# Output projection of a hybrid decoder layer as seven block products instead of eight, with weight sums made by adding transfers

## The chip, the cores and the metric

The kernel runs on one core of a Trainium2 chip. TensorE (PE in the profile) multiplies, VectorE (DVE), ScalarE (ACT) and GpSimd (POOL) work on vectors, SyncE (SP) issues transfers. The metric is the device time of one execution in microseconds (us), lower is better. POOL can issue transfers too, and those may add to what lies at their destination.

## The reference

One layer with 512 tokens of width 1024, float32. What matters here is the end of the mixer and the start of the MLP:

```python
merged = jax.nn.sigmoid(gate_attn) * attn + jax.nn.sigmoid(gate_conv) * conv
x = x + merged @ w_out[l]

hmid = jnp.square(jax.nn.relu(rms_norm(x, norm_mlp_g[l]) @ w_ff1[l]))
x = x + hmid @ w_ff2[l]
```

`attn` is a projection by `w_attn_o`, `conv` one by `w_conv_out`; `merged` is 512 x 1024, `w_out` 1024 x 1024, `w_ff1` 1024 x 4096 and `w_ff2` 4096 x 1024.

## The kernel before

Every float32 product is done in three passes of a rounded format (fp32r): a matrix is split in a high half (ACT copies it with rounding) and a low half (the difference, a subtraction on DVE or POOL), and high x high, high x low and low x high are summed in PSUM. A weight chunk thus needs one ACT and one DVE or POOL instruction of 128 x 1024 for each 512 KB that a transfer brings.

The order of the work is written out by hand. `at(pos, fn, ...)` files a step under a position; all steps are sorted by it and issued in that order, and each engine runs its own part of them as an in-order queue. One unit of position is six matmuls of 512 columns. `WO` is where the projection by `w_attn_o` starts, `WC` that by `w_conv_out`, `W0` the output projection by `w_out`, `M0` the MLP.

- **Merge** (`wc_evac`, L629 to L634). For each 128 of the 1024 features, DVE multiplies and adds in PSUM (L630, L631), ACT rounds half of it to the high half `mT["h"]` (L632), DVE makes the low half (L633).
- **Output projection** (L1006 to L1077). It is plain: first the left 512 output columns for all four token tiles at once (`wout_first`), then the right ones tile by tile (`wout_second`), 96 matmuls each. The weights come in four chunks in the ring of the buffer tag `raw`; the low halves are made by POOL for the first two pieces and by DVE afterwards (L465).
- **Residual and norm.** `residual` adds the projection to `x1` on DVE, `residual_square` sums the squares on ACT, `x2_norm` (L1039) makes the root of the mean and the normed tile `u` on DVE, with short instructions of one column in between (L1041, L150, L127 to L130) and one long one (L1045). `x2_trans` transposes `u` on PE, `x2_keep` copies it to `cx`, the MLP's operand. The tiles `x1` are loaded at `WO + 3` (L993).
- **MLP** (L1089 to L1341). Eight phases, `w_ff1` and `w_ff2` in turn for a quarter of the hidden width. Each phase is a 1024 x 1024 product in 2 x 2 blocks of 512, in Winograd's form with seven products instead of eight. `piece_hi` and `piece_lo` (L1134 to L1139) split the weight blocks on ACT and DVE, `products` (L1152) issues the matmuls, `op_sum`, `op_hi` and `op_lo` make the sums and halves of the other operand, `row_add` (L1171) adds a product to `x1`. Weight sums are made by DVE (`block_sum`, L1130) or by transfers that add (`fetch_add`, L1116, issued by POOL). Phase 0 starts with products 1 and 2, which need token tiles 0 and 1 only, then product 7, which needs all four.

Four weight blocks are held (`raw` in `tl`) and four pieces (`ph`, `pl`); piece `n` goes to place `n % 4`, so its high half waits until TensorE has finished with piece `n - 4`.

Of the kernel before, what the change touches and what calls it, by code (L numbers as in the profile page):

```python
# [53 lines left out]
def tile_hybrid_block(  # L54
# [220 lines left out]
    kw = [gpool.tile([P, KD, 256], F32R, name=f"kw{i}", tag="gate", bufs=2) for i in range(2)]  # L275
# [188 lines left out]
    def split_lo(u):  # L464
        eng = ve if u in wout_uses[2:] else ge  # L465
        eng.tensor_tensor(out=pieces[u][1], in0=piece_of(u), in1=pieces[u][0].bitcast(F32), op=ALU.subtract)
# [147 lines left out]
    for name, c0, tag, res in (("ta", GLU_END, "gate", ta), ("tc", GA_END, "kT", tcv)):  # L614
        at(b + 3.9, gate_tiles, name, tag, res)
# [7 lines left out]
    aTh, mT = {}, {}  # L623
    M_SHAPE = [P, 2, S]
# [4 lines left out]
    def wc_evac(ps, m):  # L629
        ve.scalar_tensor_tensor(out=ps, in0=tcv[m], scalar=1.0, in1=ps, op0=ALU.add, op1=ALU.mult)  # L630
        ve.tensor_tensor(out=ps, in0=ta[m], in1=ps, op=ALU.add)  # L631
        se.activation(mT["h"][:, m, :], ps, AF.Copy, scale=0.5)  # L632
        ve.scalar_tensor_tensor(out=mT["l"][:, m, :], in0=ps, scalar=0.5, in1=mT["h"][:, m, :].bitcast(F32),  # L633
                                op0=ALU.mult, op1=ALU.subtract)  # L634
# [320 lines left out]
    def merge_tiles():  # L955
        for n in "hl":
            mT[n] = keep.tile([P, KD, S], F32R, name=f"mT{n}", tag="act", bufs=2)

    at(WC, merge_tiles)


    W0 = WC + 4 * KD
    M0 = W0 + 32
    tl = {}

    def open_tail():
# [4 lines left out]
        tl["raw"] = [pool.tile([P, 4, S], F32, name=f"block{i}") for i in range(2)]  # L971
        for n in "hl":
            tl["p" + n] = [pool.tile([P, 2, S], F32R, name=f"piece{n}")]
        tl["u2"] = pool.tile([P, 2, D], F32, name="u2", tag="aOh")
# [6 lines left out]
        for n in "hl":  # L981
            tl["wout" + n] = pool.tile([P, KD, S], F32R, name=f"wout1{n}", tag="xS" + n)
# [7 lines left out]
    def load_x1():  # L990
        for t in range(NT):
            x1_t = keep.tile([P, D], F32, name=f"x1_{t}", tag="at", bufs=4)
            nc.sync.dma_start(x1_t, x[t * P:(t + 1) * P, :])  # L993
            x1.append(x1_t)

    at(WO + 3, load_x1)
# [9 lines left out]
    def wout_mm(acc, k, t, wh, wl):  # L1006
        cols = slice(t * P, (t + 1) * P)
        mm_M(acc, mT["h"][:, k, cols], mT["l"][:, k, cols], wh, wl, k == 0, k == KD - 1)

    def wout_first(u, i, j):  # L1010
        if i + j == 0:
            tl["acc"] = [bank(f"ps_wo0_{t}") for t in range(NT)]
        wh, wl = pieces[u]
        for t in range(NT):
            wout_mm(tl["acc"][t], 2 * i + j, t, wh[:, j, :], wl[:, j, :])

    def wout_second(t, i):
        if i == 0:
            tl["acc", t] = bank(f"ps_wo1_{t}")
        for k in (2 * i, 2 * i + 1):  # L1020
            wout_mm(tl["acc", t], k, t, tl["wouth"][:, k, :], tl["woutl"][:, k, :])

    def wout_hi(m):
        se.copy(tl["wouth"][:, 2 * m:2 * m + 2, :], raws[wout_late[m // 2]][:, 2 * (m % 2):2 * (m % 2) + 2, :])

    def wout_lo(m):
        ks = slice(2 * m, 2 * m + 2)
        ve.tensor_tensor(out=tl["woutl"][:, ks, :], in0=raws[wout_late[m // 2]][:, 2 * (m % 2):2 * (m % 2) + 2, :],
                         in1=tl["wouth"][:, ks, :].bitcast(F32), op=ALU.subtract)

    def residual(t, half, acc):
        cols = slice(half * S, half * S + S)
        ve.tensor_tensor(out=x1[t][:, cols], in0=x1[t][:, cols], in1=acc, op=ALU.add)

# [4 lines left out]
    def x2_norm(t):  # L1039
# [3 lines left out]
        rs = rsqrt_root(root[t], mean_eps(ss, D, 1, f"m{t}"), 1, f"m{t}")  # L1043
# [393 lines left out]
```

## Time and profile before

| | us |
|---|---|
| median of 3 runs | 768.29 |
| the runs | 766.93, 768.29, 1067.66 |
| span of the profiled execution | 766.8 |
| output projection starts | 401.49 |
| MLP's phase 0 starts | 448.44 |
| MLP's phase 2 starts | 528.87 |
| merge's eight instructions each, ACT L632 and DVE L633 | 0.60 and 0.69 |

The profiled execution's span is 0.1 us below the lowest run and 1.5 below the median; the third run was disturbed. Starts are counted from the span's start. In the profile's rows a name like `ps_x<-xSh,pieceh` says what an instruction writes and reads, with buffer numbers left out; L1163 is the line of the matmuls of a `w_ff1` phase, L1168 that of a `w_ff2` phase.

### The profile page before, as it was taken

The page shows a single profiled execution, that of the slowest core. Times are in us where ns is not written, and L with a number is a line of the kernel's source. Part 1 is how long each engine was busy: PE and PEld are TensorE (multiplying, and loading weights), DVE is VectorE, ACT ScalarE, POOL GpSimd, SP SyncE. Part 2 cuts the span into 40 slices and gives each one's busy share as a digit, 9 for nine tenths or more (in the row PEclk, how much of TensorE's full clock was granted, in tenths as well). Part 3 has the DMA queues.
Part 4 walks back from the last instruction along what each step waited for, and adds up shares of the span by engine and source line. Part 5 has one row for each costly group of instructions (what it writes and reads, how often), then busy time and mean ns, then how long its engine had stood idle before and what let it go on. Part 6 is the DMA issues. An engine that isn't in the chain of part 4 may idle for free.

```text
span 766.8 us, 11628 instructions
## 1 busy us (share of the span) xinstructions
PE 758.6 (99%) x4468; PEld 667.5 (87%) x4468; DVE 604.4 (79%) x926; ACT 439.8 (57%) x697; POOL 275.8 (36%) x215
## 2 busy tenths in 40 slices
PE   9999999999999999999999999999999999999997
PEld 8989989898888888888888899979998899889986
DVE  5467978898878888888436678899779977998696
ACT  7445457667566656348325367754675467536761
POOL 1454978958675475524440002210121011101110
PEclk9999999999999999999999999999999999999999
DMA  7441051313223113533228207983588359844772
GB/s 260 157 146 56 1 165 31 108 56 120 73 78 117 56 57 109 168 108 101 104 70 302 82 29 140 218 204 98 150 208 193 110 135 218 179 129 119 166 157 109
DMA packets 65870, 97.48 MB, mean 127 GB/s; under 512 B 3524, under 2 KB 36340, under 8 KB 65814
## 3 DMA queue, kind: packets, MB, share of 16 engines
q1 hardware_dynamic: 56566, 78.91, 30.9%
q0 software_dynamic: 9248, 17.83, 13.7%
q8 instruction: 35, 0.57, 0.3%
q14 instruction: 21, 0.17, 0.1%
HBM read 94.60 MB, written 2.12 MB: 126 GB/s over the span
## 4 chain that ended last, share of the span: by engine, by line
PE 85%; DVE 5%; ACT 3%; DMA 3%; POOL 2%; issue 2%; POOLq 0%; ACTq 0%; DVEq 0%
PE ps_x L1163 10%; PE ps_z L1168 8%; PE ps_y L1163 5%; PE ps_y L1168 4%; PE ps_x L1168 3%; PE ps_z L1163 2%; DMA block<-in_w_ff_dram 2%; PE ps_ta L498 2%; PE ps_ta L500 2%; PE ps_wo L198 2%; PE ps_wo L199 2%; PE ps_wo L197 2%; PE ps_ta L499 2%; PE ps_wc L500 2%; PE ps_wc L499 2%; PE ps_wc L498 2%
## 5 line engine op out<-in xcount | busy, mean ns | idle before, releaser
L1138 DVE TENSOR_TENSOR piecel<-block,pieceh 128x1024 fp32r<-128x1024 f32 x112 | 136.2, 1223 | 33.5 <-ACT pieceh L1135 33.4
L1135 ACT CAST pieceh<-block 128x1024 fp32r<-128x1024 f32 x112 | 116.0, 1050 | 71.4 <-DVE block L1132 21.4
L1118 POOL DMA_DIRECT2D block<-in_w_ff_dram x34 | 41.3, 1249 | 296.9 <-DVE piecel L1138 173.1
L800 DVE SCALAR_TENSOR_TENSOR cv<-h,wcol,cv 128x512 f32<-128x512 f32 x208 | 147.7, 748 | 0.5
L1163 PE MATMUL ps_x<-xSh,pieceh 128*128 128x256 f32 x192 | 54.1, 282 | 0.4 <-ACT c L1182 0.4
L1163 PE MATMUL ps_x<-xSl,pieceh 128*128 128x256 f32 x192 | 53.9, 281 | 0.0
L1163 PE MATMUL ps_x<-xSh,piecel 128*128 128x256 f32 x192 | 53.9, 281 | 0.0
L709 ACT ACTIVATE s<-s,negm 128x257 f32<-128x257 f32 (+1 forms) x64 | 30.4, 480 | 16.5 <-DVE negm L701 16.5
L1168 PE MATMUL ps_z<-piecel,aSh 128*128 128x512 f32 x96 | 37.8, 394 | 0.9 <-DVE piecel L1138 0.8
L733 DVE TENSOR_TENSOR pTl<-ptp,pTh 128x512 fp32r<-128x512 f32 x28 | 19.4, 691 | 23.0 <-ACT pTh L729 23.0
L1168 PE MATMUL ps_z<-pieceh,aSh 128*128 128x512 f32 x96 | 37.5, 390 | 0.0
L1168 PE MATMUL ps_z<-pieceh,aSl 128*128 128x512 f32 x96 | 37.4, 390 | 0.0
L1132 DVE TENSOR_TENSOR block<-block,block 128x1024 f32<-128x1024 f32 x30 | 36.6, 1224 | 0.8 <-DMA block<-in_w_ff_dram 0.4
L1163 PEld LDWEIGHTS ps_x<-xSh,piecel 128*128 128x128 f32 x192 | 36.8, 192 | 0.0
L197 PE MATMUL ps_q<-wh_q,uTh 128*128 128x256 f32 x128 | 36.6, 286 | 0.0
L1163 PEld LDWEIGHTS ps_x<-xSh,pieceh 128*128 128x128 f32 x192 | 36.0, 188 | 0.6 <-ACT c L1182 0.6
L199 PE MATMUL ps_q<-wh_q,uTl 128*128 128x256 f32 x128 | 36.2, 283 | 0.0
L198 PE MATMUL ps_q<-wl_q,uTh 128*128 128x256 f32 x128 | 36.2, 283 | 0.0
L1163 PEld LDWEIGHTS ps_x<-xSl,pieceh 128*128 128x128 f32 x192 | 36.1, 188 | 0.0
L792 POOL TENSOR_TENSOR side<-side,tap 128x512 f32<-128x512 f32 x24 | 31.1, 1295 | 13.6 <-ACT tap L791 13.6
L1202 ACT CAST aSh<-c 128x1024 fp32r<-128x1024 f32 x16 | 16.8, 1050 | 28.8 <-DVE c L1216 13.1
L718 POOL TENSOR_TENSOR s<-s,r 128x1024 f32<-128x1024 f32 (+1 forms) x16 | 26.9, 1682 | 14.7 <-DVE r L713 14.7
(324 smaller groups left out, 2541.2 us busy)
## 6 DMA issues: line engine op xcount, KB each, us to landing
block<-in_w_ff_dram SPq DMA_DIRECT2D x64, 512.0 KB, 5.4
block<-in_w_ff_dram POOLq DMA_DIRECT2D x34, 512.0 KB, 6.6
x<-in_x_dram SPq DMA_DIRECT2D x8, 512.0 KB, 5.1
raw_g<-in_w_in_dram SPq DMA_DIRECT2D x8, 512.0 KB, 4.5
raw_a<-in_w_in_dram SPq DMA_DIRECT2D x8, 512.0 KB, 3.5
raw_q<-in_w_in_dram SPq DMA_DIRECT2D x8, 512.0 KB, 5.6
raw_ta<-in_w_in_dram SPq DMA_DIRECT2D x8, 512.0 KB, 4.4
raw_tc<-in_w_in_dram SPq DMA_DIRECT2D x8, 512.0 KB, 3.5
```

The lines of the kernel that those rows point to most:

```text
L197: pe.matmul(ps, ah, wh, start=first, stop=False)
L198: pe.matmul(ps, ah, wl, start=False, stop=False)
L199: pe.matmul(ps, al, wh, start=False, stop=last)
L498: pe.matmul(ps, wh[:, k, :], ah(k), start=(k == 0), stop=False)
L792: ge.tensor_tensor(out=side[ct], in0=side[ct], in1=tap, op=ALU.add)
L800: ve.scalar_tensor_tensor(out=cps[ct], in0=src, scalar=w, in1=cps[ct], op0=ALU.mult, op1=ALU.add)
L1118: ge.dma_start(tl["raw"][buf][:, ks, :], block(ph, i, j)[:, ks, :], accum_op=ALU.add)
L1132: ve.tensor_tensor(out=o, in0=a, in1=b, op=ALU.add)
L1135: se.copy(tl["ph"][n % 4], tl["raw"][buf][:, 2 * h:2 * h + 2, :])
L1138: ve.tensor_tensor(out=tl["pl"][n % 4], in0=tl["raw"][buf][:, 2 * h:2 * h + 2, :], in1=tl["ph"][n % 4].bitcast(F32), op=ALU.subtract)
L1163: pe.matmul(o, b[:, c, w], a[:, k, :], start=(first and c + q + i == 0), stop=(k == 3 and i == 2), skip_group_check=True)
L1168: pe.matmul(acc, a[:, k, w], b[:, c, :], start=(first and c + i == 0), stop=(k == 3 and i == 2), skip_group_check=True)
```

## The change

The output projection becomes a phase -1 of the MLP's scheme: seven block products of 24 matmuls each of 512 columns, in the order 1, 2, 6, 5, 3, 7, 4, and `M0` moves from `W0 + 32` to `W0 + 28`.

`merged` is no longer split at the merge; it stays as float32 in the gate tiles `ta`, which move to the pool `keep` so that they live on, and is cut into four blocks `cm`. `operands("m", ...)` makes their sums on DVE and their halves on ACT and DVE. The weight blocks of `w_out` are fetched and summed by adding transfers, ten of them new on POOL's queue. `x1` is loaded by `open_tail`, behind the first blocks on SP's queue. Fourteen low halves (`POOL_LO`: ten of the projection's, the first four of phase 0) and four block sums of phase 0 are made by POOL. `x2_norm` is cut in two steps, and the square-root table is loaded earlier.

```diff
 def wc_evac(ps, m):
     ve.scalar_tensor_tensor(out=ps, in0=tcv[m], scalar=1.0, in1=ps, op0=ALU.add, op1=ALU.mult)
-    ve.tensor_tensor(out=ps, in0=ta[m], in1=ps, op=ALU.add)
-    se.activation(mT["h"][:, m, :], ps, AF.Copy, scale=0.5)
-    ve.scalar_tensor_tensor(out=mT["l"][:, m, :], in0=ps, scalar=0.5, in1=mT["h"][:, m, :].bitcast(F32),
-                            op0=ALU.mult, op1=ALU.subtract)
+    ve.tensor_tensor(out=ta[m], in0=ta[m], in1=ps, op=ALU.add)
...
-    def gate_tiles(name, tag, res):
-        tiles = [gpool.tile([P, NG, S], F32, name=f"{name}_{i}", tag=tag, bufs=2) for i in range(2)]
+    def gate_tiles(name, pool, tag, res):
+        tiles = [pool.tile([P, NG, S], F32, name=f"{name}_{i}", tag=tag, bufs=2) for i in range(2)]
         res += [tiles[m // 4][:, m % 4, :] for m in range(KD)]
+        if name == "ta":
+            tl["cm"] = [tiles[k][:, :, 256 * i:256 * i + 256] for i in range(2) for k in range(2)]
...
+    for i, ch in enumerate(ring[-2:]):
+        at(last_of[ch], lambda i=i: open_block(i))
...
+        for t in range(NT):
+            x1_t = pool.tile([P, D], F32, name=f"x1_{t}")
+            nc.sync.dma_start(x1_t, x[t * P:(t + 1) * P, :])
+            x1.append(x1_t)
...
+    def x2_root(t):
         ss = tl["ssm"][:, t, 0:1]
         ve.tensor_tensor(out=ss, in0=ss, in1=tl["ssm"][:, t, 1:2], op=ALU.add)
         se.activation(root[t], ss, AF.Sqrt, scale=1.0 / D, bias=epsc)
-        rs = rsqrt_root(root[t], mean_eps(ss, D, 1, f"m{t}"), 1, f"m{t}")
+        tl["ms", t] = mean_eps(ss, D, 1, f"m{t}")
+
+    def x2_norm(t):
+        rs = rsqrt_root(root[t], tl["ms", t], 1, f"m{t}")
...
+    at(W0 - 6, lambda: se.activation(roots[:, 0:1], epsc, AF.Sqrt))
     for t in range(NT):
+        e, n = W0 + (18.1, 20.1, 26.1, 28.1)[t], W0 + (20.2, 22.3, 27.4, 29.5)[t]
+        at(W0 + (13.6, 14.6, 22.4, 24.4)[t], residual_square, t, t // 2)
+        at(e + 0.3, residual_square, t, 1 - t // 2)
+        at(e + 0.8, x2_root, t)
+        at(n, x2_norm, t)
         for half in range(2):
+            at(n + (2.1, 2.1, 2.5, 3.3)[t] + 0.2 * half, x2_trans, t, half)
+            at(n + (2.4, 2.4, 2.8, 3.4)[t] + 0.4 * half, x2_keep, t, half)
...
+    ORDER = [(1, 2, 7, 6, 5, 4, 3)] + [(1, 7, 6, 2, 5, 4, 3)] * (PHASES - 1) + [(1, 2, 6, 5, 3, 7, 4)]
...
     def home(ph, prod):
+        if ph < 0:
+            return {1: 0, 5: 0, 2: 1, 7: 1, 6: 2, 4: 2, 3: 3}[prod]
...
+    def open_block(buf):
+        raw = wp.tile([P, 4, S], F32, name=f"block{buf}", tag="raw", bufs=2)
+        tl["raw"][buf] = [raw[:, 2 * h:2 * h + 2, :] for h in range(2)]
+        for h in range(2):
+            fetch(-1, buf, buf, 0, h)
...
+    def block_sum(out, a, b, h, eng=ve):
+        o, a, b = (tl["raw"][i][h] for i in (out, a, b))
+        eng.tensor_tensor(out=o, in0=a, in1=b, op=ALU.add)
...
     def piece_lo(n, buf, h):
-        ve.tensor_tensor(out=tl["pl"][n % 4], in0=tl["raw"][buf][:, 2 * h:2 * h + 2, :],
+        (ge if n in POOL_LO else ve).tensor_tensor(out=tl["pl"][n % 4], in0=tl["raw"][buf][h],
                          in1=tl["ph"][n % 4].bitcast(F32), op=ALU.subtract)
...
     def operand(ph, prod):
+        if ph < 0:
+            return [v[:, {7: 0, 6: 1, 4: 1, 5: 2, 2: 2, 3: 3, 1: 3}[prod]] for v in tl["mS"]]
...
+        if x == "m":
+            ve.scalar_tensor_tensor(out=lo, in0=tl["cm"][SRC[prod]], scalar=0.5, in1=hi.bitcast(F32),
+                                    op0=ALU.mult, op1=ALU.subtract)
...
+    POOL_LO = {-14, -13, -12, -9, -7, -5, -4, -3, -2, -1, 0, 1, 2, 3}
...
+    operands("m", {"P1": WC + 18, "S3": WC + 20, "P7": WC + 21, "P2": W0 + 1.3, "S2": W0 + 2.2, "P6": W0 + 2.9,
+                   "S1": W0 + 5, "P5": W0 + 8.1, "S4": W0 + 10.5, "P3": W0 + 11.6, "P4": W0 + 14.4})
     for h in range(2):
+        at(WO + 3.1 + 0.1 * h, fetch, -1, 2, 0, 0, h)
+        at(WO + 3.3 + 0.1 * h, fetch, -1, 3, 1, 1, h)
+        at(WO + 14 + h, fetch_add, -1, 2, 0, 1, h)
+        at(WO + 24 + h, fetch_add, -1, 2, 1, 1, h)
+    for j, prod in enumerate(ORDER[-1]):
+        p = W0 + 4 * j
+        for h in range(2):
+            n = 2 * (j - 7) + h
+            s = {-14: W0 - 7.8, -13: W0 - 3.8, -12: W0 + 0.3, -11: W0 + 1.1}.get(n, p - 4.9 + h)
+            at(s, piece_hi, n, home(-1, prod), h)
+            at(s + 0.75, piece_lo, n, home(-1, prod), h)
+            for t in range(2):
+                at(p + 2 * t + h, products, -1, prod, n, h, t)
+            d = s + 0.9
+            if prod == 1:
+                at(d, fetch_add, -1, 0, 0, 1, h)
+            elif prod == 2:
+                at(d, fetch, -1, 1, 0, 1, h)
+                at(d + 6, fetch_add, -1, 1, 1, 1, h)
+            elif prod == 6:
+                at(d + 3, fetch_add, -1, 2, 1, 0, h)
+            else:
+                at(d, fetch, 0, home(-1, prod), *{5: (0, 0), 3: (1, 0), 7: (0, 1), 4: (1, 1)}[prod], h)
+        for t in range(2):
+            half_t, half_n, minus = {1: (0, 0, 0), 7: (1, 1, 1), 6: (1, 0, 0), 2: (0, 0, 0),
+                                     5: (1, 1, 1), 4: (1, 0, 0), 3: (0, 1, 1)}[prod]
+            at(p + 2.1 + 2 * t, row_add, -1, half_t, half_n, prod, t, minus, 0)
...
+                    q1, q3, q2, q4 = m - 2.9 + h, m - 1.4 + h, m + 5.2 + 1.7 * h, m + 10.2 + 0.9 * h
                 at(q1, block_sum, h11, h11, ht, h)
+                at(q3, block_sum, ht, ht, h22, h, ve if ph else ge)
+                at(q2, block_sum, ht, h11, h22, h, ve if ph else ge)
```

More of the change, by code (lines that the diff above doesn't have):

```diff
@@ L274, in tile_hybrid_block @@
     ssk = sm.tile([P, 16], F32, name="ssk", tag="ss16")
-    kw = [gpool.tile([P, KD, 256], F32R, name=f"kw{i}", tag="gate", bufs=2) for i in range(2)]
+    kw = [keep.tile([P, KD, 256], F32R, name=f"kw{i}", tag="gate", bufs=2) for i in range(2)]
     def heads_raw(ps, raw, ss, t):
@@ L395, in k_hi @@
             k2["h"] = att.tile([P, 16, 2, HD], F32R, name="k2h", tag="qs")
-            k2["l"] = gpool.tile([P, 16, 2, HD], F32R, name="k2l", tag="gate", bufs=2)
+            k2["l"] = keep.tile([P, 16, 2, HD], F32R, name="k2l", tag="gate", bufs=2)
         se.copy(k2["h"][:, :, j, :], k3)
@@ L464, in split_lo @@
     def split_lo(u):
[L465 to L466 removed]
+        ge.tensor_tensor(out=pieces[u][1], in0=piece_of(u), in1=pieces[u][0].bitcast(F32), op=ALU.subtract)
     pool_of = {"mm": ps1}
@@ L613, in tile_hybrid_block @@
         (glu_tile if part[0] == "h" else q_group)(int(part[1]))
-    for name, c0, tag, res in (("ta", GLU_END, "gate", ta), ("tc", GA_END, "kT", tcv)):
-        at(b + 3.9, gate_tiles, name, tag, res)
+    for name, c0, pool, tag, res in (("ta", GLU_END, keep, "gate", ta), ("tc", GA_END, gpool, "kT", tcv)):
+        at(b + 3.9, gate_tiles, name, pool, tag, res)
         for m in range(0, KD, 2):
@@ L621, in tile_hybrid_block @@
                 b += 4
-    aTh, mT = {}, {}
-    M_SHAPE = [P, 2, S]
+    aTh = {}
     def wo_evac(ps, m):
@@ L953, in tile_hybrid_block @@
         at(p + 3.0, silu_lo, ct)
[L955 to L963, printed above, removed]
+    M0 = W0 + 28
     tl = {}
@@ L970, in open_tail @@
         tl["pool"] = pool
[L971 to L974, printed above, removed]
         cx = pool.tile([P, 2, 4, 256], F32, name="cx1", tag="aOl")
         tl["cx"] = [cx[:, i] for i in range(2)]
-        tl["ca"] = [pool.tile([P, 4, 256], F32, name=f"c{i}") for i in range(4)]
+        tl["u2"] = pool.tile([P, 2, D], F32, name="u2", tag="aOh")
+        for t in range(NT):
+            x1_t = pool.tile([P, D], F32, name=f"x1_{t}")
+            nc.sync.dma_start(x1_t, x[t * P:(t + 1) * P, :])
+            x1.append(x1_t)
+        for n in "hl":
+            tl["p" + n][1] = pool.tile([P, 2, S], F32R, name=f"piece{n}")
         gmlp = tl["gmlp"] = pool.tile([P, D], F32, name="gmlp", tag="aEh")
@@ L980, in open_tail @@
         pool.tile([P, 48], F32, name="shift")
-        for n in "hl":
-            tl["wout" + n] = pool.tile([P, KD, S], F32R, name=f"wout1{n}", tag="xS" + n)
+        tl["xS"] = [pool.tile([P, 4, 4, 256], F32R, name=f"xS{n}") for n in "hl"]
         tl["xE"] = [pool.tile([P, 4, 256], F32R, name=f"xE{n}") for n in "hl"]
@@ L988, in tile_hybrid_block, with open_merge, open_early, open_c @@
     x1 = []
[L990 to L996, printed above, removed]
+    def open_merge():
+        tl["mS"] = [keep.tile([P, 4, 4, 256], F32R, name=f"mS{n}", tag="act", bufs=2) for n in "hl"]
+        for n in "hl":
+            tl["p" + n] = [None] * 4
+    def open_early():
+        tl["raw"] = [None] * 4
+        for buf in (3, 2):
+            tl["raw"][buf] = [keep.tile([P, 2, S], F32, name=f"block{buf}{h}", tag="at", bufs=4) for h in range(2)]
+    def open_c():
+        tl["ca"] = []
+        for _ in range(2):
+            c = keep.tile([P, 2, 4, 256], F32, name="ca", tag="gate", bufs=2)
+            tl["ca"] += [c[:, i] for i in range(2)]
+    at(WO + 3, open_early)
+    at(WC + 0.1, open_merge)
     at(W0 + 0.9, open_tail)
+    at(W0 + 20, open_c)
     banks = ["ln", "ln", "ln", "mm", "mm", "mm"]
@@ L1004, in bank @@
         return pool_of["mm"].tile([P, S], F32, name=name, tag=banks[-1])
[L1006 to L1033, printed above, removed]
     def residual_square(t, half):
@@ L1229, in open_x @@
         tl["cx"] += [cx[:, i] for i in range(2)]
-        tl["xS"] = [tl["pool"].tile([P, 4, 4, 256], F32R, name=f"xS{n}", tag="xS" + n) for n in "hl"]
     def open_a(what):
@@ L1239, in open_banks @@
     def open_banks():
-        x, y, z = ([bank(f"ps_{role}{t}") for t in range(2)] for role in "xyz")
+        z, x, y = ([bank(f"ps_{role}{t}") for t in range(2)] for role in "zxy")
         tl["banks"] = ({"x": x, "y": y, "z": z}, {"x": z, "y": y, "z": x})
```

81 lines of the change are left out of this document (17 added, 64 removed).

## The prediction

> **What bounds the kernel now.** I read the page's head first, then the chain that ended last, then the stretches around the output projection, then the engines' queues there.
>
> ```profile
> span 766.8 us, 11628 instructions
> PE 758.6 (99%) x4468; PEld 667.5 (87%) x4468; DVE 604.4 (79%) x926; ACT 439.8 (57%) x697; POOL 275.8 (36%) x215
> PEclk9999999999999999999999999999999999999999
> ```
>
> TensorE is busy 99% of the span at full clock, so time goes where matmuls go, unless a new wait opens. In the chain (start, length):
>
> ```profile
> 436.02 0.87 PE tp_m L1052 x8
> ...
> 448.44 5.66 PE ps_x L1163 x48
> ...
> 507.11 5.44 PE ps_x L1168 x24
> ...
> 528.87 5.65 PE ps_x L1163 x48
> ```
>
> One block product costs 5.44 us where the weights move 512 wide (24 matmuls) and 5.65 in the other form (48). The stretches:
>
> ```profile
> 401.49:423.25 21.76, 21.76 (x97) 18.02 (x96) 15.61 (x16) 11.09 (x14) 0.23 (x1) 1.00 0.80 284
> 423.25:448.44 25.19, 25.19 (x123) 20.62 (x122) 16.19 (x32) 10.76 (x24) 0.00 (x0) 1.00 0.20 69
> 448.44:528.87 80.43, 79.30 (x514) 71.98 (x514) 71.88 (x77) 52.26 (x61) 12.31 (x10) 1.00 0.67 157
> ```
>
> The output projection is the first two rows: 96 matmuls in 21.76 us, then 96 and three sets of transposes in 25.19. PE never stops there, and POOL does nothing after 401.7. Phases 0 and 1 of the MLP hold 7 x 5.65 + 7 x 5.44 + 0.87 = 78.50 us of 80.43, so 1.93 us of waiting, which I keep.
>
> **What comes off.** 192 matmuls in 46.95 - 3 x 0.87 = 44.34 us become 168, seven products of 5.44 = 38.08. That is 6.26 us less: 766.8 - 6.26 = 760.54. From here on the question is only whether PE still finds its operands.
>
> **What the change puts on the other engines.** Rows for the new instructions:
>
> ```profile
> L1138 DVE TENSOR_TENSOR piecel<-block,pieceh 128x1024 fp32r<-128x1024 f32 x112 | 136.2, 1223 | 33.5 <-ACT pieceh L1135 33.4
> L1135 ACT CAST pieceh<-block 128x1024 fp32r<-128x1024 f32 x112 | 116.0, 1050 | 71.4 <-DVE block L1132 21.4 <-DMA block<-in_w_ff_dram 15.4 <-PE ps_x L1163 13.7
> L466 POOL TENSOR_TENSOR wl_wc<-raw_wc,wh_wc 128x1024 fp32r<-128x1024 f32 x8 | 19.2, 2398 | 24.2 <-ACT wh_wc L462 24.2
> L1173 DVE TENSOR_TENSOR x<-x,ps_z 128x512 f32<-128x512 f32 x32 | 20.6, 683 | 3.8 <-PE ps_z L1168 3.8
> L1045 DVE SCALAR_TENSOR_TENSOR u<-x,roots,gmlp 128x1024 f32<-128x1024 f32 x4 | 5.1, 1286 | 0.1
> L1118 POOL DMA_DIRECT2D block<-in_w_ff_dram x34: 1203/1210/1907, 462.9 to 738.7; - x34
> ```
>
> Ten of the 14 low halves of the projection's pieces and the first four of phase 0 go to POOL at 2.40 us (DVE: 1.22), as do four block sums of phase 0. That these run beside DVE without cost must be read from a place where both engines worked:
>
> ```profile
> 313.22 2.84 POOL L466 TENSOR_TENSOR wl_wo<-raw_wo,wh_wo 128x1024 fp32r<-128x1024 f32 x1 [1.80 <-ACT wh_wo L462]
> 313.72 0.75 DVE L800 SCALAR_TENSOR_TENSOR cv<-h,wcol,cv 128x512 f32<-128x512 f32 x1
> 314.38 2.77 DVE L862 TENSOR_TENSOR aTl<-attnT,aTh 128x1024 fp32r<-128x1024 f32 x1
> L862 DVE TENSOR_TENSOR aTl<-attnT,aTh x4: 1212/1222/2767, 311.4 to 317.1; 128x1024 fp32r<-128x1024 f32 x4
> 24.84 1.28 DVE L300 SCALAR_TENSOR_TENSOR u<-x,roots,gmix 128x1024 f32<-128x1024 f32 x1
> 25.11 3.27 POOL L466 TENSOR_TENSOR wl_g<-raw_g,wh_g 128x1024 fp32r<-128x1024 f32 x1 [13.61 <-ACT wh_g L462]
> 335.25 2.55 POOL L466 TENSOR_TENSOR wl_wo<-raw_wo,wh_wo 128x1024 fp32r<-128x1024 f32 x1 [0.23 <-ACT wh_wo L462]
> 336.91 0.91 DVE L112 TENSOR_SCALAR y_ln<-ms_ln 128x4 int32<-128x4 int32 x1
> 337.86 0.17 DVE L113 TENSOR_SCALAR y_ln<-y_ln 128x4 int32<-128x4 int32 x1
> ```
>
> This is the view that decides. A DVE instruction with both inputs in SBUF, started at 314.38 inside a POOL subtraction that ended at 316.06, took 2.77 us instead of 1.22: it stood until POOL was done. At 25.11 it is POOL that stands until DVE's 1.28 is over (3.27 instead of 2.40). Even a 128x4 DVE instruction of 0.17 us became 0.91, ending with POOL's at 337.8. So such instructions take turns, whole ones at a time. DVE's row additions read PSUM and are free of it: L800, one input in PSUM, ran its usual 0.75 at 313.72.
> The Trainium skill, SBUF — State Buffer, section "SBUF: two separate sides", says so: one port pair, held for a whole instruction, the other fully blocks; these rows agree.
>
> Now the sum over that turn-taking, from the projection's start (W0 = 0 us) to phase 0's third product, which needs the last transposes: 38.08 + 2 x 5.65 + 4 x 0.87 = 52.9 us without waits. POOL has 12 low halves and 2 block sums, 14 x 2.3 = 32 us (held time, from 313.7 to 316.0). DVE has about 23 instructions of 128x1024 with two SBUF inputs (4 low halves, 5 low halves and 3 sums of merged, 4 x u, 4 low halves and 1 sum in phase 0, 2 block sums), at 1.14 a turn 26 us, and some 25 short ones, 2 us. 60 us do not fit into 51.6 (POOL begins at 1.3): at least 8.8 us of waiting even if packed without a gap.
>
> **The queues walked by hand** (positions in the code order each engine's queue; DVE 1.2, POOL 2.4, ACT 1.0, row additions 0.65; us after W0). Product 2 (5.4) is in time: P2's low half ends at 5.9, held up by POOL's first low half until 3.6. Product 6: DVE is at it until 11.1, so POOL's second low half runs 11.1 to 13.5, wanted at 12.6: 0.9 wait. Product 5: four accumulating transfers stand in POOL's queue ahead of its low half, 4 x 1.21, so it runs 18.3 to 20.8, wanted at 19.3: 1.5, and 0.3 for P5, whose sum S1 waited for POOL until 13.4. Product 3: 0.8. Product 7: 0.4. Together 4.0.
> Then the norms. Each token tile needs a sum, a mean, a reciprocal, three products and u: seven turns, each short, against a POOL that has subtractions queued.
>
> ```profile
> 430.59 0.16 DVE L1041 TENSOR_TENSOR ssm<-ssm 128x1 f32<-128x1 f32 x1 [0.85 <-ACT fsq L1036]
> ...
> 431.11 0.16 DVE L127 RECIPROCAL roots<-roots 128x1 f32<-128x1 f32 x1 [0.17 <-ACT roots L1042]
> ...
> 431.90 1.29 DVE L1045 SCALAR_TENSOR_TENSOR u<-x,roots,gmlp 128x1024 f32<-128x1024 f32 x1
> ```
>
> Now it takes 430.59 to 433.2, 2.6 us. Tile 0: begun at 30.3, but three POOL subtractions (to 37.5) slip in between, u is ready at 39.4, and PE, which has the transposes in its queue behind the third quarter of product 7, arrives at 35.4: 4.1 wait. Tile 1: 0 or 3.9, by which of u and POOL's next subtraction comes first (0.3 us decide); I take 0. Tile 2: behind POOL's low half, block sum and low half in a row (3 x 2.4 after q1's second half), u comes 7.7 after PE. Tile 3 and P7: 0.9. The sum is 4.0 + 4.1 + 0 + 7.7 + 0.9 = 16.7, so 760.54 + 16.7 = 777.2. I take 777, nearer to the walk than to the packed bound, since queues are in order and the bound leaves no gap (760.5 + 8.8 = 769.3).
>
> **Edits with small or no cost.**
>
> ```profile
> L633 DVE SCALAR_TENSOR_TENSOR mTl<-ps_wc,mTh 128x512 fp32r<-128x512 f32 x8 | 5.5, 692 | 5.3 <-ACT mTh L632 5.3
> L632 ACT ACTIVATE mTh<-ps_wc x8: 597/598/600, 365.1 to 403.2; 128x512 fp32r<-128x512 f32 x8
> 388.45 2.39 POOL L466 TENSOR_TENSOR wl_wc<-raw_wc,wh_wc 128x1024 fp32r<-128x1024 f32 x1 [3.05 <-ACT wh_wc L462]
> 312.70 5.94 SPq L993 DMA_DIRECT2D x<-in_x_dram  x4
> 401.69 0.70 DVE L630 SCALAR_TENSOR_TENSOR ps_wc<-tc,ps_wc 128x512 f32<-128x512 f32 x1 [2.66 <-PE ps_wc L500]
> x<-in_x_dram SPq DMA_DIRECT2D x8, 512.0 KB, 5.1
> DMA to landing us min/median/max: 5.5/6.6/14.4
> ```
>
> Eight ACT copies (0.60) and eight DVE subtractions (0.69) leave the merge: free, PE covers them. The x loads move from 312.7 behind two w_out blocks on SP, the later of which waits for its space until 388.45 + 2.39 = 390.8. Their own memory is the convolution's, long unused, so they land by about 400, ahead of the first row addition at 404.4: nothing. If SP had to wait for the last merge (401.69 + 1.4), the first lands near 408.2, row addition and everything behind it on DVE (S2, P6) come 2 us later: 2 us more, not less. Accumulating transfers: ten new on POOL, 1.21 each, four of them priced above, the other six in idle stretches; they land in 6.6 us (14.4 at most), and product 5's block is wanted 11 us after its issue: 0 to 3 us, I take 0. The square-root table comes earlier, into idle ACT: nothing. Gate tiles in another pool, banks in another order: nothing moves in the queues.
> The Trainium skill, the same page and section, also has a trap: while DVE holds the pair, POOL cannot write a transfer's descriptors, and 0.62 us became 3.1. Here 34 issues beside a busy DVE took 1.20 to 1.91, median 1.21; so I don't stretch them, and by the page's figure four in a row would, as an estimate, cost up to 7.6 us more, ending near 785.
>
> **Rivals.**
> 1. The turns bite little (other side: faster). If DVE's waiting instruction keeps its place for the whole short chain, the norms slip through between two POOL subtractions, and only the queue term of 1.5 and about 1 us at the last transposes stay: 760.5 + 2.5 = 763. For it: the short ones last 0.16 us. Against it: L112's 0.91, and 60 us for 51.6. It decides if a tile's chain, 430.59 to 433.2 now, stays under 4 us.
> 2. Worse turns. Tile 1's 3.9 falls due, and in phase 0 the two POOL sums before piece 6 (2.4 instead of 1.22) hold up S2, P6 and P7's low halves, 2 x 2.4: 777.2 + 3.9 + 4.8 = 786. The four issues at the slowest row's 1.91 would add 2.8 in the same place. For it: POOL back to back; against it: later PE means POOL waits for pieces too.
> 3. The x loads late: 777 + 2 = 779; it lies within the forecast's own range.
>
> **How the numbers follow.** The profiled execution (766.8 span; the lowest run is 766.93) stands 1.4 below the median of 768.29; a median may come out that much higher. Forecast 777, its own range 769 (packed) to 783 (tile 1 late and x late): 0.57. Rival 1, 763: 0.25. Rival 2, 786: 0.18. For 8 in 10 the range takes rival 1 in and stops short of rival 2: 762 to 785. Two per cent, about what a measurement of this kernel can tell from no change, is 15.4 us, 752.9 to 783.7: faster 0.01 (all 6.26 and the 1.93 of old waits would not do it), slower 0.21 (rival 2 and the end of the range), same 0.78.
>
> **What would show it.** Seven products of 5.44 in the projection: the 6.26. Low halves on POOL, 14 of them near 2.4 or above; DVE groups of two SBUF inputs with maxima of 2.5 to 3.6 instead of 1.23; short norm instructions with maxima above 1 us; PE waits in front of tp_m, released by u, of 4 and about 8 us: the walk. POOL's third low half behind four issues, PE waiting for it: the 1.5. Wrong if DVE's maxima stay at 1.3 in this stage, if tp_m waits for nothing, or if PE's new waits sit at transfers.

## The result, and the profile after

| | before | after |
|---|---|---|
| median | 768.29 us | 788.85 us (788.20 to 789.21, 5 runs) |
| profiled execution, its span | 766.8 us | 787.0 us |
| ratio | 1 | 1.0274 [1.0261, 1.0287] |

The change makes the kernel 2.7% slower. The ratio leaves out the disturbed run of the kernel before (1067.66 us), so it is not exactly the quotient of the two medians. The forecast of 777 is 11.9 us too low, and the time lies 3.9 us above the upper end of its range. From the page of the kernel after: the span, the engines' busy time, TensorE's granted clock in 40 slices, and three groups with their busy time and mean ns of one.

```profile
span 787.0 us, 11652 instructions
...
PE 759.1 (96%) x4444; PEld 666.5 (85%) x4444; DVE 633.7 (81%) x925; ACT 448.1 (57%) x702; POOL 328.4 (42%) x241
...
PEclk9999999999999999999998889999999999999999
...
L1089 DVE TENSOR_TENSOR piecel<-block,pieceh 128x1024 fp32r<-128x1024 f32 x112 | 144.6, 1297 | 32.0 <-ACT pieceh L1086 31.8
...
L1089 POOL TENSOR_TENSOR piecel<-block,pieceh 128x1024 fp32r<-128x1024 f32 x14 | 35.0, 2541 | 25.1 <-ACT pieceh L1086 25.1
...
L1083 DVE TENSOR_TENSOR block<-block,block 128x1024 f32<-128x1024 f32 x26 | 35.5, 1365 | 0.4
```

TensorE went from 99% to 96% of a longer span. The low halves on VectorE (L1089) have a mean of 1297 ns where it was 1223, and the clock shows three slices below 9, which it did not before. Both lie in one stretch. The next rows are the stretch from the start of the output projection to the end of the MLP's phase 1, in the kernel before and in the kernel after (length, then busy time with count for PE, PEld, DVE, ACT, POOL, then granted clock, DMA share, GB/s).

```profile
401.49:528.87 127.38, 126.25 (x731) 110.63 (x730) 103.67 (x123) 74.11 (x97) 12.54 (x11) 1.00 0.60 161
```

```profile
403.10:549.71 146.61, 126.51 (x707) 109.55 (x706) 130.36 (x126) 82.70 (x105) 57.95 (x30) 0.94 0.61 149
```

146.61 - 127.38 = 19.2 us more, and the stretch begins 403.10 - 401.49 = 1.6 us later: 20.8, which is the whole difference (20.56 by the medians). The saving of 6.26 is in it: there are 24 x 7 matmuls in the projection, 0.227 us apart at full clock. So some 26.8 us were lost against a projection without waits. TensorE's waits over the whole span (total, times, longest):

```profile
PE tp_m L1020 <- DVE u L1013: 8.3, 1, 8.3
PE ps_z L1121 <- DVE x L1126: 3.7, 2, 2.6
PE ps_z L1121 <- POOL piecel L1089: 2.8, 2, 2.2
PE tp_m L1020 <- DVE ssm L1006: 2.7, 1, 2.7
PE ps_y L1116 <- DVE xSl L1163: 1.8, 1, 1.8
```

All of these are new, and in this stretch none of TensorE's waits ends with a transfer. The row that names ssm is tile 0's: its u ends at 446.71 and its transposes start at 446.86. The longest wait is that of the transposes of tile 2, and the timeline shows where it comes from (start, length, engine, line; every fence of a timeline below has these columns):

```profile
457.13 2.83 DVE L1083 TENSOR_TENSOR block<-block,block 128x1024 f32<-128x1024 f32 x1
...
458.83 3.33 POOL L1089 TENSOR_TENSOR piecel<-block,pieceh 128x1024 fp32r<-128x1024 f32 x1
...
459.88 2.29 DVE L1006 TENSOR_TENSOR ssm<-ssm 128x1 f32<-128x1 f32 x1
462.12 2.34 POOL L1083 TENSOR_TENSOR block<-block,block 128x1024 f32<-128x1024 f32 x1
...
462.21 0.15 DVE L150 TENSOR_SCALAR ms_m<-ssm 128x1 f32<-128x1 f32 x1
...
462.73 1.75 DVE L128 TENSOR_TENSOR a_m<-roots 128x1 f32<-128x1 f32 x1
464.42 2.34 POOL L1089 TENSOR_TENSOR piecel<-block,pieceh 128x1024 fp32r<-128x1024 f32 x1
464.51 2.26 DVE L129 SCALAR_TENSOR_TENSOR a_m<-a_m,ms_m 128x1 f32<-128x1 f32 x1
...
467.00 1.28 DVE L1013 SCALAR_TENSOR_TENSOR u<-x,roots,gmlp 128x1024 f32<-128x1024 f32 x1
...
468.43 1.09 PE L1020 MATMUL tp_m<-ident,u 128*128 128x128 f32 x4 [8.32 <-DVE u L1013]
```

The three short VectorE instructions of 128x1 with two SBUF inputs (0.16 us before) took 2.29, 1.75 and 2.26 us, and each ends where an instruction of POOL ends (462.16, 464.46, 466.76). The short one with one tensor input (L150) took its 0.15 in the middle of it. This is the mechanism of the prediction, at the place it named. A second place was not named:

```profile
422.06 1.20 POOL L1069 DMA_DIRECT2D block<-in_w_out_dram  x1 [2.07 <-issue]
...
422.55 6.52 DVE L1089 TENSOR_TENSOR piecel<-block,pieceh 128x1024 fp32r<-128x1024 f32 x1
...
422.81 5.17 POOL L1089 TENSOR_TENSOR piecel<-block,pieceh 128x1024 fp32r<-128x1024 f32 x2
...
425.70 0.50 PE L1121 MATMUL ps_z<-piecel,mSh 128*128 128x512 f32 x1 [2.21 <-POOL piecel L1089]
...
426.74 0.39 PE L1121 MATMUL ps_z<-pieceh,mSl 128*128 128x512 f32 x1
428.99 0.67 DVE L1126 TENSOR_TENSOR x<-x,ps_z 128x512 f32<-128x512 f32 x1
...
429.72 0.80 PE L1121 MATMUL ps_z<-pieceh,mSh 128*128 128x512 f32 x1 [2.60 <-DVE x L1126]
430.31 0.63 PE L1121 MATMUL ps_z<-piecel,mSh 128*128 128x512 f32 x1
...
430.74 0.63 PE L1121 MATMUL ps_z<-pieceh,mSl 128*128 128x512 f32 x1
```

A low half on VectorE (1.22 us alone) stood through two POOL subtractions in a row, 6.52 us, although its record begins 0.26 us ahead of theirs; it ends at 429.07, 1.09 us after the second of them. Behind it in VectorE's queue is the row addition of product 6, and product 5 accumulates in the PSUM bank which that addition has to read first, so TensorE stood as well. And when it went on at 429.72, its matmuls were 0.43 us apart (430.31 to 430.74) instead of 0.227, until 433.7. The same slow spacing follows the waits of tile 0 and tile 2. Last, the 1.6 us by which the projection starts late come from the layer norm far ahead of it:

```profile
335.15 2.58 POOL L1069 DMA_DIRECT2D block<-in_w_out_dram  x2
...
336.85 3.31 POOL L457 TENSOR_TENSOR wl_wo<-raw_wo,wh_wo 128x1024 fp32r<-128x1024 f32 x1
...
337.10 3.10 DVE L112 TENSOR_SCALAR y_ln<-ms_ln 128x4 int32<-128x4 int32 x1
```

Two of the new adding transfers stand in POOL's queue ahead of a weight subtraction, which so starts at 336.85 instead of 335.25; the 128x4 instruction of the layer norm's chain falls into it whole, 3.10 us instead of 0.91.

### The profile page after: what moved, and what is told of

Same layout as the page of the kernel before. It is cut to its first block, busy times and chain, and to the rows that moved or that the text cites. A ratio compares the mean times of both kernels' runs of the same rounds, so it can differ in the third digit from the quotient of the medians.

```text
span 787.0 us, 11652 instructions
## 1 busy us (share of the span) xinstructions
PE 759.1 (96%) x4444; PEld 666.5 (85%) x4444; DVE 633.7 (81%) x925; ACT 448.1 (57%) x702; POOL 328.4 (42%) x241
## 4 chain that ended last, share of the span: by engine, by line
PE 86%; DVE 8%; ACT 2%; POOL 2%; issue 1%; DMA 1%; DVEq 0%; POOLq 0%; ACTq 0%
PE ps_z L1121 12%; PE ps_x L1116 11%; PE ps_y L1116 6%; PE ps_y L1121 6%; PE ps_x L1121 3%; PE ps_z L1116 2%; PE ps_ta L489 2%; PE ps_ta L491 2%; PE ps_ta L490 2%; PE ps_wc L490 2%; PE ps_wc L489 2%; PE ps_wc L491 2%; PE ps_tc L489 2%; PE ps_tc L491 2%; PE ps_tc L490 2%; PE ps_g L489 2%
## 5 line engine op out<-in xcount | busy, mean ns | idle before, releaser
L1086 ACT CAST pieceh<-block 128x1024 fp32r<-128x1024 f32 x126 | 129.9, 1045 | 86.6 <-DVE block L1083 19.1
L1089 DVE TENSOR_TENSOR piecel<-block,pieceh 128x1024 fp32r<-128x1024 f32 x112 | 144.6, 1297 | 32.0 <-ACT pieceh L1086 31.8
L1089 POOL TENSOR_TENSOR piecel<-block,pieceh 128x1024 fp32r<-128x1024 f32 x14 | 35.0, 2541 | 25.1 <-ACT pieceh L1086 25.1
L1155 ACT ACTIVATE aSh<-ca 128x1024 fp32r<-128x1024 f32 x16 | 16.9, 1056 | 28.7 <-DVE ca L1173 13.1
```

The lines of the kernel that those rows point to most:

```text
L1086: se.copy(tl["ph"][n % 4], tl["raw"][buf][h])
L1089: (ge if n in POOL_LO else ve).tensor_tensor(out=tl["pl"][n % 4], in0=tl["raw"][buf][h], in1=tl["ph"][n % 4].bitcast(F32), op=ALU.subtract)
```

## The experiments

The main theory: POOL's new arithmetic (14 low halves, 4 block sums) and VectorE's instructions with two SBUF inputs exclude one another; without POOL's share most of the loss goes. The rivals: VectorE is simply full, so that taking work back onto it costs as much; or the loss lies in transfers or in TensorE's clock.

**1. No arithmetic of the change on POOL (e1).**

```diff
-    POOL_LO = {-14, -13, -12, -9, -7, -5, -4, -3, -2, -1, 0, 1, 2, 3}
+    POOL_LO = set()
...
-                at(q3, block_sum, ht, ht, h22, h, ve if ph else ge)
-                at(q2, block_sum, ht, h11, h22, h, ve if ph else ge)
+                at(q3, block_sum, ht, ht, h22, h)
+                at(q2, block_sum, ht, h11, h22, h)
```

> All 14 low halves and the four block sums go from POOL to DVE; POOL keeps only its transfers. Theory T (turns: a POOL instruction that reads SBUF and a DVE instruction with two SBUF inputs exclude each other for whole instructions, and PE's new waits come from that): although DVE gets 18 instructions of 1.22 us more, no DVE instruction of that stage takes over 1.3 us, the waits at the transposes shrink, the time falls to 765 to 777. Rival Q (queue: DVE simply has too much in its in-order queue in this stage, POOL relieves it): up to 18 x 1.22 us more, 789 to 811.

Measured: 773.97 us, ratio 1.0073 [1.0058, 1.0088], so 14.9 us come off the kernel after although VectorE has 18 instructions more. The form of the low halves (min/median/max) and the two longest new waits of TensorE, of e1:

```profile
L1089 DVE TENSOR_TENSOR piecel<-block,pieceh x126: 1216/1220/1227, 393.3 to 761.9; 128x1024 fp32r<-128x1024 f32 x126
```

```profile
PE tp_m L1020 <- DVE u L1013: 4.1, 2, 3.7
PE ps_z L1121 <- DVE x L1126: 2.0, 1, 2.0
```

No low half takes longer than 1.23 us any more. The two longest waits left are on VectorE's queue: tile 2's u behind block sums and a low half, and product 6's row addition.

**2. The short instructions with one SBUF tensor input (e2).** The other factor is given as a per-partition scalar:

```diff
-        ve.tensor_tensor(out=a, in0=y, in1=y, op=ALU.mult)
+        ve.tensor_scalar(out=a, in0=y, scalar1=y, scalar2=-0.5, op0=ALU.mult, op1=ALU.mult)
...
-        ve.tensor_tensor(out=ss, in0=ss, in1=tl["ssm"][:, t, 1:2], op=ALU.add)
+        ve.tensor_scalar(out=ss, in0=ss, scalar1=tl["ssm"][:, t, 1:2], scalar2=None, op0=ALU.add)
```

> As the changed kernel, but the short norm instructions of one column (sum of the two squares, the three Newton steps) take the second operand as a per-partition scalar, so that each has one SBUF tensor input. Nothing else moves. T: those that took 1.75 to 2.30 us go back to 0.16, the norms of tiles 0 and 2 come 3 to 6 us earlier each, the time falls by 5 to 9 us to 780 to 784, and the long u instruction may still wait once per tile. Q: 788 to 789, nothing changes, as their number and work are the same.

Measured: 784.29 us, ratio 1.0207 [1.0192, 1.0222], 4.6 us less than after, a little under the 5 to 9 expected. The end of tile 2's chain in e2:

```profile
458.23 0.21 DVE L130 TENSOR_SCALAR a_m<-a_m,ms_m 128x1 f32<-128x1 f32 x1
458.48 0.21 DVE L131 TENSOR_SCALAR roots<-roots,a_m 128x1 f32<-128x1 f32 x1
458.73 1.85 DVE L1018 SCALAR_TENSOR_TENSOR u<-x,roots,gmlp 128x1024 f32<-128x1024 f32 x1
```

A POOL subtraction ran from 456.17 to 459.49; the short ones pass beside it in 0.21 us, and u, which has two SBUF tensors, waits. The wait ahead of tile 2's transposes is 3.8 us instead of 8.3, the same 4.5 as the gain. The Trainium skill, SBUF — State Buffer, section "Who interferes with whom", says that a VectorE instruction with at most one SBUF input (outside the modes that use both ports) is free of POOL; these rows agree.

**3. The same conflict put into the kernel before (e3), and POOL busy without reading SBUF (e4).** Both add unused work on POOL ahead of each tile's norm: e3 two subtractions, e4 one instruction of 128x1 and six fills.

```diff
+    def idle_pool(t, i):
+        ge.tensor_tensor(out=tl["scr"], in0=x1[t], in1=x1[t], op=ALU.subtract)
...
+        for i in range(2):
+            at(e + 0.12, idle_pool, t, i)
```

> The kernel before with two extra POOL subtractions of 128x1024 per token tile, placed after its second residual, reading x1 and writing a scratch tile that nobody reads: eight in all. No queue of DVE, ACT or SP gets anything, no data depends on them. T: the norm's short instructions and u stretch to 1 to 3.5 us, each tile's u comes 3 to 4.6 us later, PE waits at the transposes, the time rises by 5 to 15 us to 772 to 783. Q: 767 to 769, as DVE's queue is the same.

> The kernel before with POOL kept busy at the same places by filling the scratch tile (six fills of 128x1024 per token tile, after a one-column instruction that ties them to the residual); they read nothing from SBUF. T: 767 to 769, no DVE instruction stretched, since only a POOL instruction that reads SBUF excludes DVE. Rival A (any POOL activity disturbs DVE): as the kernel with the subtractions, 772 to 783. Q: 767 to 769.

Measured: e3 773.33 us, ratio 1.0067 [1.0052, 1.0082]; e4 768.23, ratio 0.9999 [0.9989, 1.0008]. The norm's first short instruction (min/median/max), first in e3, then in e4:

```profile
L1042 DVE TENSOR_TENSOR ssm<-ssm x4: 1141/1204/1267, 430.7 to 454.1; 128x1 f32<-128x1 f32 x4
```

```profile
L1042 DVE TENSOR_TENSOR ssm<-ssm x4: 159/160/160, 430.5 to 450.1; 128x1 f32<-128x1 f32 x4
```

Eight POOL subtractions whose result nobody reads cost 5.5 us in a kernel that has none of the change (773.33 - 767.79, the kernel before on that chip). 3.3 us of that are TensorE's two new waits ahead of tp_m, 1.7 the slow spacing behind the first. Fills, 5.7 us a tile against the subtractions' 3.8, cost nothing. So it is POOL's reading of SBUF, not POOL being busy, that stops VectorE.

**4. The four early adding transfers later (e5).**

```diff
-        at(WO + 14 + h, fetch_add, -1, 2, 0, 1, h)
-        at(WO + 24 + h, fetch_add, -1, 2, 1, 1, h)
+        at(WO + 34 + h, fetch_add, -1, 2, 0, 1, h)
+        at(WO + 44 + h, fetch_add, -1, 2, 1, 1, h)
```

> As the changed kernel, with only the four adding transfers of the stage of the projection by w_attn_o issued 20 positions later on POOL, in the stage of the projection by w_conv_out. T: two of them put off a POOL subtraction until it lay over a 128x4 DVE instruction of the layer norm (3.10 us instead of 0.91 before); without them that one is back at about 0.9, the output projection starts 1.2 to 1.7 us earlier, 787.1 to 787.7. Rival: the start is late for another cause (tiles in another place, transfers): 788.9, same start.

Measured: 788.04 us (783.64 to 789.29), ratio 1.0253 [1.0226, 1.0279]. The layer norm's instruction is back at 0.91 us, and the projection's first wait comes 1.7 us earlier (413.67 instead of 415.42), the last 1.4 us earlier (479.36 instead of 480.78). Then the gain is gone. The next rows are two neighbouring intervals of 3.41 us around that last wait, first in after, then in e5 (columns as in the stretches above; TensorE's busy time is the first number behind the length, the clock the third from the end):

```profile
478.21:481.63 3.42, 2.17 (x17) 1.78 (x16) 2.30 (x3) 1.96 (x2) 3.05 (x1) 1.00 0.00 0
481.63:485.04 3.41, 2.04 (x17) 2.04 (x18) 3.38 (x3) 0.84 (x2) 0.23 (x1) 1.00 0.00 0
```

```profile
478.08:481.49 3.41, 1.60 (x12) 1.20 (x10) 2.29 (x2) 1.99 (x2) 2.38 (x1) 1.00 0.00 0
481.49:484.90 3.41, 3.30 (x15) 3.31 (x16) 3.38 (x5) 1.99 (x2) 0.56 (x1) 0.50 0.00 0
```

A wait of the same length (2.22 and 2.24 us from matmul to matmul) is followed by full clock in one execution and by half clock in the other, which costs 1.4 us. What differs is where the wait lies. In after the granted clock changes at 427.01, 433.84, 447.50, 450.91, 464.56 and 471.39, always a whole multiple of 3.41 us apart, and so it does in the traces of all the other runs. In after the wait lies across a border of two such intervals and leaves 2.17 and 2.04 us of work in them; in e5 it lies almost whole in one and leaves 1.60, and the next one has half clock. The run of 783.64 us had a mean granted clock of 0.993, the other three 0.986 to 0.987. So the transfers' price is real, 1.6 us at the start, but what the clock makes of the waits behind can take it away again.

**5. TensorE kept busy in the two long waits (e6, e11).** Unused matmuls of 128x128 ahead of the transposes of tiles 0 and 2: 24 and 72 in e6, 12 and 36 in e11.

```diff
+        if half == 0 and t in (0, 2):
+            for _ in range(12 if t == 0 else 36):
+                pe.matmul(tp[:, 0, :], ident, ident, start=True, stop=True)
```

> As the changed kernel, with 24 and 72 matmuls of 128x128 that nobody reads put on TensorE's queue ahead of the transposes of tiles 0 and 2, where it waits 2.9 and 8.5 us. They fill the waits and end none. Theory C (part of the loss is TensorE's clock, which falls behind a long wait: matmuls at 0.43 us instead of 0.227): the matmuls behind the two waits run at full pace, the time falls by 1.5 to 4 us to 785 to 787.4. Rival: the slow ones only hide in waits that come anyway: 788.2 to 789.5; if the filler takes longer than the waits, up to 792.

> The kernel after with 12 and 36 unused 128x128 matmuls ahead of the first transposes of tiles 0 and 2, so that TensorE has work during most of the two long waits there. Theory (the matmuls at 0.43 us spacing behind the waits are the price of TensorE having stood still): the spacing behind both waits is 0.23 from the start, 1.7 and 0.7 us less: 785.5 to 787.5. Rival (the slow spacing comes from elsewhere, or the filler costs as much as it saves): 788 to 790, with the spacing of 0.43 still there behind tile 0.

Measured: e6 794.87 us, ratio 1.0354 [1.0340, 1.0368]; there the filler outlasted the waits, so it says nothing of the clock's price. e11: 791.41, ratio 1.0290 [1.0272, 1.0307]. Stretches of e11, the third number from the end is the clock:

```profile
444.40:450.00 5.60, 5.60 (x42) 5.12 (x41) 5.35 (x11) 2.77 (x7) 2.65 (x2) 1.00 0.61 184
...
460.00:470.00 10.00, 9.95 (x89) 9.76 (x88) 8.77 (x10) 2.39 (x5) 6.68 (x3) 1.00 0.33 107
...
480.00:500.00 20.00, 17.66 (x124) 17.47 (x125) 16.61 (x15) 12.85 (x16) 6.46 (x5) 0.83 0.64 122
```

The filler does what it should: the clock stays at 1.00 behind both waits (after: 0.91 from 440 to 460, 0.83 from 460 to 480). But my expectation fell. The first matmul with a low half in product 7 of phase 0 begins at 482.72, where it was 483.00: TensorE arrives earlier and only waits longer there, because VectorE and POOL set that time. Behind that wait the clock is now the lower one (after: 1.00 from 480 to 500), and nothing is won: 1.0290 beside 1.0274. (The rival fell too: it had the slow spacing stay behind tile 0.) The slow spacing is caused by TensorE standing still; keeping it busy pays only where TensorE sets the pace.

**6. VectorE's queue in another order (e7, e8, e9, e12).** All have e1's and e5's edits. e7 also moves a row addition of product 6, block sums and low halves. e8 is e7 with u computed on ScalarE. In both, the transfer of the next block was put ahead of product 5's second low half, which so splits the next block's data: that product is another one than the reference's.

> No POOL arithmetic in the stage, the four adding transfers later, and on DVE's queue four things in another order: piece -10 ahead of P6, the row addition of product 6 ahead of its neighbour's low half, the second halves of the block sums behind tile 2's norm, and tile 2's transposes at the end of product 1. T and the queue's order: of the 774.0 of the kernel without POOL arithmetic the start (1.2), the wait for the row addition (2.0), tile 2 (3.7) and the slow clock behind these (2 to 3) go, 764 to 768. If DVE's sum of work bounds the stage whatever the order: 771 to 774.

> As the reordered one, and the norm's long instruction (1.29 us per tile) goes from DVE to ACT: ACT scales the tile by the root, and the gain is applied by ACT in the copies behind the transposes, four of 128 columns instead of one of 512. DVE loses 5.2 us, ACT gains about 7. T with DVE as the stage's bound: 761 to 766, below the kernel before. If ACT becomes late instead: 767 to 772.

Measured: e7 781.72, e8 783.93 us. TensorE waited about 8 us for that low half in both, since it now waited for the transfer: they show the price of that misplacement and nothing else. e9 has the transfer behind the low half, and goes on (the main lines):

```diff
-            at(s + 0.75, piece_lo, n, home(-1, prod), h)
+            at(s + (1.0 if n == -7 else 0.75), piece_lo, n, home(-1, prod), h)
...
-            d = s + 0.9
+            d = s + (1.15 if n == -7 else 0.9)
...
-            at(p + 2.1 + 2 * t, row_add, -1, half_t, half_n, prod, t, minus, 0)
+            at({(6, 0): W0 + 9.05, (4, 1): W0 + 27.25}.get((prod, t), p + 2.1 + 2 * t), row_add, -1, half_t, half_n, prod, t, minus, 0)
...
-                    q1, q3, q2, q4 = m - 2.9 + h, m - 1.4 + h, m + 5.2 + 1.7 * h, m + 10.2 + 0.9 * h
+                    q1, q3, q2, q4 = m - 2.9 + 3.8 * h, m + 1.0 + 0.6 * h, m + 5.2 + 1.7 * h, m + 10.2 + 0.9 * h
```

> The kernel after with all low halves and block sums on DVE (as in e1), the four early adding transfers 20 places later (as in e5), and DVE's queue put in another order: the low half for product 5 goes behind the first row addition of product 6; the second row addition of product 4, the norms of tiles 2 and 3 and the operand of phase 0's second product go ahead of the block sums. Theory (what e1 still lost was the order of DVE's queue and the start, not the amount of work): against 773.97 of e1 the start comes 1.2 us earlier, and row addition (2.0), the slow matmuls after it (1.7) and tile 2 (3.7) go: 761 to 767, below the kernel before. Rival (DVE is simply full there, so the waits only move): 771 to 776, with waits of PE on DVE of 3 us or more between 440 and 485.

Measured: 773.96 us, ratio 1.0064 [1.0049, 1.0079]: the rival's number. The waits on u and on the row addition shrank to 1.1 and 0.9, and a longer one took their place, in e9:

```profile
PE tp_m L1020 <- ACT cx L1024: 6.9, 2, 6.1
```

ScalarE stood at the high half of a piece whose block sum VectorE had not done, with the copies of the transposed tile behind it. e12 puts those high halves and block sums behind the copies:

> e9 with one more change of order: ScalarE's high halves for phase 0's pieces 4 to 6 and DVE's second block sums go behind the copies of tiles 2 and 3 and behind the first block sum of x, so that ScalarE no longer stands at a piece whose block sum is not done while the transposed tile waits to be copied. Theory (e9's 6.4 and 1.9 us ahead of tile 3's transposes were ScalarE's queue, and DVE has just enough room): those 8.3 us and about 1.5 us of slow matmuls behind them go, some 2.5 us come up in front of product 7 of phase 0, whose low halves are now the last of DVE's queue: 773.96 - 9.8 + 2.5 = 766.7, between 764 and 769, level with the kernel before. Rival (DVE is full from 445 on, so the wait only moves to product 7): 771 to 775, with one wait of 5 us or more in front of product 7.

Measured: 770.68 us, ratio 1.0031 [1.0020, 1.0043], the fastest kernel with the change, and still 2.3 us above the kernel before. Its waits:

```profile
PE ps_y L1116 <- DVE piecel L1089: 1.9, 1, 1.9
PE tp_m L1020 <- DVE u L1013: 1.8, 2, 1.1
PE ps_x L1116 <- ACT ca L1135: 1.5, 1, 1.5
...
PE ps_z L1121 <- DVE piecel L1089: 1.0, 2, 0.6
PE ps_z L1121 <- DVE x L1126: 0.9, 1, 0.9
```

Between the two expectations: the long wait went and none of 5 us came up, but five small ones stay. The stretches of e12 from 440 on (VectorE's busy time is the third after the length):

```profile
440.00:460.00 20.00, 18.27 (x135) 16.48 (x133) 19.17 (x30) 13.12 (x24) 0.00 (x0) 1.00 0.15 54
460.00:480.00 20.00, 17.28 (x132) 16.89 (x133) 19.37 (x18) 13.91 (x17) 4.88 (x4) 0.91 0.54 101
```

VectorE is busy 19.2 and 19.4 of 20 us. The five waits sum to 7.1 us, and the clock of 0.91 in the second row takes some 1.7 more. So the rival is right as a limit, as far as these orders show: once POOL's arithmetic is back on it, VectorE has next to no room left in this stage, and the projection's 6.26 us are eaten in small waits. Whether u on ScalarE (e8's idea) would make room in e12's order was not run.

## Why the prediction was wrong

Its main step held. One block product is 5.44 us, seven of them save 6.26, and VectorE's two-input instructions exclude POOL's reading ones; e1, e3 and e4 show that directly. The stage's loss was taken from the right mechanism and came out too small. Its terms, from the starts of the matmuls (start to start less the regular spacing):

| the prediction's term | us | measured |
|---|---|---|
| product 6 | 0.9 | 0.74 |
| product 5 | 1.5 + 0.3 | 1.24 + 2.37 + 2.75 |
| product 3, product 7 | 0.8 + 0.4 | 0 |
| tile 0 | 4.1 | 2.86 |
| tile 1 | 0 | 0 |
| tile 2 | 7.7 | 8.49 |
| tile 3 and P7 | 0.9 | 0.95 + 2.11 |
| matmuls at low clock | not priced | 4.5 |
| later start (adding transfers at 335.15) | 0 | 1.6 |
| 1.9 of old waits | kept | gone, -1.6 |

The measured column sums to 26.0, with 0.6 of slow transposes behind tile 2's wait 26.6, against the 26.8 us that the medians show. The forecast had 16.7.

- **The step that failed most** is "Product 5: ... 1.5, and 0.3", which came to 6.36, for two reasons. "Such instructions take turns, whole ones at a time" was read from single POOL instructions; here VectorE got no turn between two (6.52 us). And the walk looked at operands only: products 6 and 5 accumulate in one bank, so product 5's two token groups wait for product 6's row additions, 1.24 and 2.75 us, and those stand behind whatever VectorE does. e9's order leaves 0.9 of it.
- **The clock.** The row of the kernel before has 1.00 everywhere, and I took the matmuls' duration as fixed. After the waits it is not: 0.43 us per 128x512 matmul at half clock, 4.5 us in all, a term that the walk put at nothing. As e11 shows, they are not 4.5 to be had back, since the next wait takes part of it.
- **"The other six in idle stretches"** was wrong for the two at 335.15: their 2.58 us shift a subtraction into the layer norm's chain. That stretch of POOL was not idle: in the kernel before the subtraction starts at 335.25, as the prediction's own rows show.
- **"Seven turns"** per norm: four, the sum, two products and u. Mean and reciprocal have one input, and the third product never waited (0.16 us in all four tiles). Tile 0 came out below its term (2.86 for 4.1), while tile 2 was longer because the block sum ahead of its chain was held up as well.
- **Tile 3 and P7**, 0.9, came to 3.06. 2.11 of it is the wait for the low half `xSl` of product 7, which stood for a POOL block sum (478.58 to 481.86) and so took 2.18 us from 480.76.
- **The second rival** gave 786, near the time, but by another sum: tile 1's 3.9 did not fall due, of its 4.8 for phase 0's POOL sums some 2 us came (the wait just named), and the 34 issues in the MLP stayed at 1.20 to 1.74 us. The Trainium skill's trap (SBUF — State Buffer, section "SBUF: two separate sides") is stated for VectorE in a mode that takes both ports of the pair; beside the two-input instructions here no issue took the 3.1 us that the prediction's estimate used. The x loads (rival 3) were never waited for. Rival 1 is excluded: tile 2's chain, to be under 4 us, took 8.4.

Still open is why VectorE got no turn between the two POOL subtractions at 422.81 and did get one in tile 2's chain, at 462.16 and 464.46. The traces show one thing that goes with it. Here VectorE's instruction began while POOL was issuing an adding transfer (422.06 to 423.26) with the subtractions right behind it; the other four kernels with such a stand have the same, and no other place in any trace has. An issue alone does not do it (the low half at 417.94 began during one and took 1.21 us). No run moves that issue alone, so it is not shown to be the cause.

## What to carry to other kernels

A saving on the engine that bounds the kernel is worth what its feeders can keep up with. In a stretch whose TensorE work shrank by 6 us, POOL's busy time grew by 45.4 us (12.54 to 57.95) and VectorE's by 26.7 (103.67 to 130.36). VectorE's growth is standing, not work: it has three instructions more (126 for 123), and thirteen of them took together some 27 us longer than their like does without POOL (6.52 for 1.22, 2.29 for 0.16). In a profile a busy engine can be one that stands. Work is only moved to POOL beside a busy VectorE if VectorE's instructions there have at most one SBUF tensor input, or POOL's read none; where that can't be, the short links of a chain can at least be written with a per-partition scalar (4.6 us here). In walking queues by hand, list for each matmul also who must have read its bank, and give waits of about 2 us and more a price for the matmuls behind them: a stretch of 3.41 us at half clock costs up to 1.7.

## What the runs showed of the hardware

- VectorE stood through two POOL subtractions in a row: a low half of 1.22 us took 6.50 to 6.85 in all five kernels that keep this order (after, e2, e5, e6, e11), each time begun during POOL's issue of an adding transfer.
- One tensor input is not free of POOL in every form: the 128x4 int32 instruction (L112) took 0.91 and 3.10 us beside a subtraction, while the 128x1 float32 one (L150) took its 0.15.
- The clock goes by fixed intervals of 3.41 us and by the work in them. In the traces of all runs, from 300 to 600 us, an interval at full clock with under 1.5 us of TensorE work was always followed by one at half clock (e1: 1.43 us in 418.93 to 422.34, 0.43 us spacing from there to 425.76), one with over 1.65 us never was (2.17 and 2.04 in after). The Trainium skill, TensorE: Matmul & The Clock Gate, section "Part 1: The HAM clock gate", has the clock halved after an idle window of about 3.4 us that runs freely; half clock (0.50 in e5's row) and the length of the interval agree, but the interval need not be idle here.
- POOL fills, which write SBUF and do not read it, left the norm's VectorE rows unchanged to 0.01 us (e4).
